# Three extra weight pairs that join a ring at the start of a stage: an encoder layer on Trainium2

## The chip, the core and the metric

The kernel runs on one core of one Trainium2 chip. The core has five engines that run at the same time, each with its own instructions in a fixed order: TensorE (PE, with its weight loads shown as PEld) multiplies matrices, VectorE (DVE) and ScalarE (ACT) work elementwise, GpSimd (POOL) does little else here than start transfers, and SyncE (SP) starts most of the transfers from memory (HBM). The metric is the time of one execution in microseconds (us).

## The reference, cut to what matters

One layer on 256 rows of width 2048: a half-weighted SwiGLU FFN of inner width 5632, a mixer (a state-space group and an attention group), a second such FFN, and a last gated stage ("ple"). What the change touches is the second FFN and the last stage:

```python
x = x + 0.5 * swiglu(rms_norm(x, ffn2_norm[i]), ffn2_w_gate[i], ffn2_w_up[i], ffn2_w_down[i])

gate = jax.nn.sigmoid(rms_norm(x, ple_norm[i]) @ w_ple_gate[i])
e = (p[i] @ w_ple_proj[i]) * gate
x = x + rms_norm(e, ple_post_norm[i])

def swiglu(h, w_gate, w_up, w_down):
    return (jax.nn.silu(h @ w_gate) * (h @ w_up)) @ w_down
```

All of it is in float32. The result has 256 x 2048 values.

## The kernel before

**A product in three passes.** TensorE takes operands of a rounded type. Each float32 matrix is therefore split in two parts: `hi`, the value cast to that type by ACT (`split`, L182), and `lo`, the rest `src - hi` by DVE (L185). A product is then `hi*hi + lo*hi + hi*lo`, three matrix multiplications. The parts of a weight are a *weight pair*: `whi` and `wlo`, each 128 x 1024 numbers, that is two blocks of 128 x 512.

**How weights come in.** A weight block of 512 x 512 (1 MB) is loaded by SP into a tile called `raw` (L369, L585). The pool `wp` has 5 such tiles; late in the kernel two of them hold the rows of x, so that three are left for weights. A load has to wait until the tile's old content has been read for the last time, which is by the DVE instruction that makes the `lo` part of its second half. Each `raw` gives two weight pairs.

**The ring.** `weight_pair` gives out the tiles for a pair. Four pairs (`whi`, `wlo`) lie in `wp`. While the list `ring` holds a pool, three more pairs (`shi`, `slo`) lie in that pool, and the seven are given out in turn: `i % 7` of 1, 3 and 5 are the extra ones. A pair can be filled again when TensorE has read its old content. When the pool of a stage closes (`sums_phase`), `ring[0]` becomes None, and pairs come from the four of `wp` alone until a stage sets the ring again. Before the change that happened in `Seven.chunk`, at the first group of seven products of a stage.

**Columns and sevens.** Much of the FFN uses a scheme that saves one product in eight (`class Seven`): a 2 x 2 block product is made from seven products of sums of blocks (`chunk`). For it DVE also adds weight blocks (`add`, L578: `t1`, `t2`, `t4`), and one sum is made by POOL as an accumulating transfer (L671). In a chunk the seven products run in the order 1, 5, 6, 4, 2, 3, 7, each with six matrix multiplications of 512 columns and one weight pair. The rest of the block product is done plainly (`column`, through `gemm_half`, L386 and L379): there a weight pair serves twelve matrix multiplications.

**The last stage.** It begins with two columns (side 0, then side 1), each with one `raw` tile, so with four weight pairs, called c1 to c4 here (c1 and c2 from `raw_2780`, c3 and c4 from `raw_2788`). Then comes one chunk, whose weights are `raw_2802` and `raw_2803`; its pairs are called z1, z5, z6, z4, z2, z3, z7 after their products, and the next columns' first pair is n1. The chunk's left operand needs sums of the normalised rows, `whole` (L507) and `rows` (L524), and their parts `hhi` and `hlo`. The normalised rows themselves come from x by a DVE transpose into `mid` (L220), 16 small transfers by SP (L233, `h<-mid`), and a scaled split (L195 on ACT, L197 on DVE). ACT also squares x (L488) and scales a gain row `pg` (L114). The second FFN begins in the same way: two columns, then a chunk.

**What sets the order.** The Python order is not what each engine gets. A scheduling layer places the instructions of each engine in an order of its own, by when it expects operands and tiles to be there; what is marked with `pin` keeps its place. Tiles of a stage's pool lie where the tiles of the pools closed before lay, and each waits until those have been read.

Of the kernel before, what the change touches and what calls it, by code (L numbers as in the profile page):

```python
# [33 lines left out]
def layer_kernel(ctx: ExitStack, tc: tile.TileContext, a: dict, shapes: dict, out: bass.AP):  # L34
# [28 lines left out]
    def uid(s):  # L63
        count[0] += 1
        return f"{s}_{count[0]}"
# [7 lines left out]
    def phase(name):  # L73
        return tc.tile_pool(name=name, bufs=1, reuse_waits="tile")
# [10 lines left out]
    def halves(kind):  # L85

        return [
            actp.tile([P, 4, T], F32R, tag=kind + s, name=uid(kind + s), bufs={"n": 4, "h": 2}[kind])
            for s in ("hi", "lo")
        ]  # L90
# [17 lines left out]
    def put_off(steps, fn, *args):  # L108


        def g():
            for _ in range(steps):
                yield
            fn(*args)  # L114

        return start(g())

    def pin(ins):
        return tc.keep_in_program_order(ins)
# [59 lines left out]
    def split(hi, lo, src, scale=None, pinned=False):  # L179

        if scale is None:
            copy = nc.scalar.copy(hi, src)  # L182
            if pinned:
                pin(copy)
            rest = nc.vector.tensor_tensor(out=lo, in0=src, in1=hi.bitcast(F32), op=ALU.subtract)  # L185
            rests.append(rest.ins)
            copies.append(copy.ins)
            return copy.ins, rest.ins
        else:
            split_each(hi.unsqueeze(1), lo.unsqueeze(1), src.unsqueeze(1), [scale])  # L190
# [149 lines left out]
    ring = [None, 0]  # L340
# [10 lines left out]
    @contextmanager  # L351
    def sums_phase(name):
        with phase(name) as pool:
            yield pool
            ring[0] = None
# [147 lines left out]
    def whole_rows(pool, parts, pinned=False):  # L503

        hi, lo = parts
        u = pool.tile([P, 2, NB], F32, tag="sum", name=uid("whole"), bufs=2)
        added = nc.vector.tensor_tensor(  # L507
            out=u.rearrange("p j n -> p (j n)"), in0=hi.bitcast(F32).rearrange("p j t -> p (j t)"),
            in1=lo.bitcast(F32).rearrange("p j t -> p (j t)"), op=ALU.add,
        )  # L510
        if pinned:
            pin(added)
        return u.rearrange("p j n -> p (j n)").rearrange("p (j x b) -> p j x b", j=4, b=32)

    def sum_forms(pool, u, kind="n"):

        sums = pool.tile([P, 2, NB], F32, tag="sum", name=uid("rows"), bufs=2)
        s = sums.rearrange("p j n -> p (j n)").rearrange("p (z j x b) -> p z j x b", z=4, j=2, b=32)
        (a11, a21), (a12, a22) = ([u[:, k : k + 2, 4 * t : 4 * t + 4] for t in range(TT)] for k in (0, 2))
        for z, (x, y, op) in enumerate((  # L520
            (a21, a22, ALU.subtract), (s[:, 0], a11, ALU.subtract),
            (a11, a21, ALU.subtract), (a12, s[:, 1], ALU.add),
        )):
            nc.vector.tensor_tensor(out=s[:, z], in0=x, in1=y, op=op)  # L524
        both = halves(kind)
        split(*both, sums.rearrange("p j n -> p (j n)").rearrange("p (z t) -> p z t", z=4))
        return both
# [175 lines left out]
    def ffn(i, xn, nxt, bg=None):  # L703
# [5 lines left out]
        sevens = pools.enter_context(sums_phase(f"sums{i}"))  # L709
        hp = pools.enter_context(phase(f"h{i}"))  # L710
        side = ExitStack()
        prep = bg(side) if bg else None
        turns = sevens
        sums = []
        mids = {}

# [13 lines left out]
        for f in range(NF):  # L730
# [3 lines left out]
            if prep and f == early:  # L734
# [3 lines left out]
                turns = pools.enter_context(phase(f"turns{i}"))  # L738
# [900 lines left out]

    n1, nm, n2, npl = Normed("ffn1_norm", load_turned), Normed("mix_norm"), Normed("ffn2_norm", kinds="hhnn", late=0), Normed("ple_norm", late=0)  # L1640
    ffn(1, n1, nm, s5_prep)

    w_in = a["w_in"]
# [75 lines left out]
    mix.close()  # L1719

    ffn(2, n2, npl)


# [27 lines left out]
    def sigmoid(sg, t, ps):  # L1751
        return nc.scalar.activation(sg[:, t * NB : (t + 1) * NB], ps, AF.Sigmoid, scale=npl.rs(t))
# [31 lines left out]
        crossed(s)  # L1784

    with sums_phase("sums3") as sevens:
        forms = {1: sum_forms(sevens, whole_rows(sevens, npl(1)), "h")}
        s = Seven(npl, forms.get, ((wg, 0), (wg, NB)), sevens, sevens)
        s.column(0, (0,))
        s.column(1, (0,))  # L1790
        s.chunk(1, shared)
        put_off(0, opened, s)
        s.column(0, (2,))
        s.column(1, (2,))
        s.column(0, (3,), True)
        put_off(0, gated, s)
        s.column(1, (3,), True)
        nc.vector.tensor_tensor(out=g1, in0=s.banks[3.8], in1=g1, op=ALU.add)
        for t in range(TT):
            sigmoid(g1, t, h1[t])  # L1800
# [180 lines left out]
```

## Time and profile before

| what | value |
| --- | --- |
| time, median of 3 runs | 1809.0 us (1808.81 to 1809.14) |
| the profiled execution | 1810.11 us, its span 1808.3 us, granted clock 0.999 |
| busy: PE, PEld, DVE, ACT, POOL | 1801.0, 1492.8, 1614.2, 1081.4, 137.1 us |
| second FFN in the trace | PE from about 1021 to 1701 us |
| last stage in the trace | PE from 1701.19 us to the end |

A start in the trace's list of instructions is counted from the beginning of the span. Two matrix multiplications of one engine overlap in such a list (each is shown as 0.39 us long, while a new one starts about every 0.227 us), so a wait of TensorE is read from the distance between starts rather than from idle time.

### The profile page before, as it was taken

How to read it: one execution, taken by the hardware profiler on the slowest of the kernel's cores; microseconds unless marked ns; L12 is line 12 of the kernel's file. 1: busy time of each engine (PE TensorE's matmuls, PEld its weight loads, DVE VectorE, ACT ScalarE, POOL GpSimd, SP SyncE). 2: the span in 40 equal slices, each digit the busy share in tenths (PEclk: the TensorE clock that was granted, in tenths of full speed). 3: DMA queues.
4: the chain of work that ended last, by engine and by line, in shares of the span. 5: the costliest groups of instructions: out<-in, count | busy, mean ns of one | idle time of the engine just before them, and what ended most of it. 6: DMA issues, size and time to landing. Idle time of an engine off the chain costs nothing.

```text
span 1808.3 us, 24274 instructions
## 1 busy us (share of the span) xinstructions
PE 1801.0 (100%) x8892; PEld 1492.8 (83%) x8892; DVE 1614.2 (89%) x1894; ACT 1081.4 (60%) x1264; POOL 137.1 (8%) x196
## 2 busy tenths in 40 slices
PE   9999999999999999999999999999999999999998
PEld 8888888888888878888898888888888888888887
DVE  7998889999999898887867899999999999989875
ACT  7445456555666566456895566555565566666664
POOL 0020100000000001112121000000000000000000
PEclk9999999999999999999999999999999999999999
DMA  9689967787776667765646777776767787666663
GB/s 377 214 277 315 279 220 234 242 268 220 257 248 228 209 237 229 258 244 179 204 153 209 248 278 239 266 263 222 233 232 248 236 273 244 231 209 221 206 245 128
DMA packets 108662, 430.49 MB, mean 238 GB/s; under 512 B 24608, under 2 KB 48576, under 8 KB 66144
## 3 DMA queue, kind: packets, MB, share of 16 engines
q1 hardware_dynamic: 96096, 390.10, 60.9%
q0 software_dynamic: 12160, 38.55, 10.0%
q8 instruction: 69, 1.13, 0.2%
q14 instruction: 49, 0.40, 0.1%
q10 hardware_dynamic: 288, 0.31, 0.1%
HBM read 372.41 MB, written 10.88 MB: 212 GB/s over the span
## 4 chain that ended last, share of the span: by engine, by line
PE 90%; DVE 4%; DMA 2%; issue 1%; SPq 1%; ACT 1%; DVEq 0%; ACTq 0%; POOL 0%; POOLq 0%
PE acc L386 29%; PE acc L379 15%; PE aux L386 13%; PE aux L379 7%; PE acc L567 5%; PE acc L572 5%; PE acc L570 5%; PE aux L570 3%; PE aux L567 3%; PE aux L572 3%; DMA raw<-in_ffn_w_down 2%; DVE wlo L185 1%; SPq L233 1%; DVE slo L185 1%; DVE sum L578 1%
## 5 line engine op out<-in xcount | busy, mean ns | idle before, releaser
L185 DVE TENSOR_TENSOR wlo<-raw,whi 128x1024 fp32r<-128x1024 f32 x478 | 576.3, 1221 | 96.7 <-ACT whi L182 94.6
L182 ACT CAST whi<-raw 128x1024 fp32r<-128x1024 f32 x478 | 495.2, 1050 | 267.2 <-PE acc L386 139.8
L386 PE MATMUL acc<-whi,nhi 128*128 128x512 f32 x850 | 331.7, 392 | 0.0
L386 PE MATMUL acc<-whi,nlo 128*128 128x512 f32 x850 | 329.7, 389 | 0.0
L379 PE MATMUL acc<-wlo,nhi 128*128 128x512 f32 x850 | 240.5, 389 | 0.1
L185 DVE TENSOR_TENSOR slo<-raw,shi 128x1024 fp32r<-128x1024 f32 x186 | 226.2, 1216 | 8.7 <-ACT shi L182 7.2
L182 ACT CAST shi<-raw 128x1024 fp32r<-128x1024 f32 x186 | 195.1, 1049 | 42.1 <-DMA raw<-in_ffn_w_down 22.5
L182 ACT CAST whi<-sum 128x1024 fp32r<-128x1024 f32 x83 | 87.5, 1054 | 168.8 <-DVE sum L578 159.3
L386 PEld LDWEIGHTS acc<-whi,nhi 128*128 128x128 f32 x850 | 159.7, 188 | 33.7 <-ACT whi L182 0.2
L379 PEld LDWEIGHTS acc<-wlo,nhi 128*128 128x128 f32 x850 | 159.4, 188 | 33.7 <-DVE wlo L185 0.5
L386 PEld LDWEIGHTS acc<-whi,nlo 128*128 128x128 f32 x850 | 159.6, 188 | 32.4
L182 ACT CAST shi<-sum 128x1024 fp32r<-128x1024 f32 x61 | 64.3, 1054 | 105.5 <-DVE sum L578 104.8
L671 POOL DMA_DIRECT2D raw<-raw x47 | 41.4, 880 | 1034.8 <-DVE sum L578 827.9
L578 DVE TENSOR_TENSOR sum<-sum,raw 128x1024 f32<-128x1024 f32 x96 | 117.1, 1220 | 0.9
L185 DVE TENSOR_TENSOR wlo<-sum,whi 128x1024 fp32r<-128x1024 f32 x83 | 101.2, 1221 | 3.1 <-ACT whi L182 2.2
L386 PE MATMUL aux<-whi,nhi 128*128 128x512 f32 x244 | 95.0, 389 | 0.0
L386 PE MATMUL aux<-whi,nlo 128*128 128x512 f32 x244 | 94.9, 389 | 0.0
L185 DVE TENSOR_TENSOR slo<-sum,shi 128x1024 fp32r<-128x1024 f32 x61 | 74.5, 1221 | 0.7
L379 PE MATMUL aux<-wlo,nhi 128*128 128x512 f32 x244 | 75.1, 389 | 0.0
L578 DVE TENSOR_TENSOR sum<-raw,raw 128x1024 f32<-128x1024 f32 x48 | 58.5, 1219 | 5.3 <-DMA raw<-in_ffn_w_down 5.2
L567 PE MATMUL acc<-whi,hhi 128*128 128x512 f32 x154 | 60.2, 391 | 0.0
L570 PE MATMUL acc<-whi,hlo 128*128 128x512 f32 x154 | 59.9, 389 | 0.0
(427 smaller groups left out, 3539.7 us busy)
## 6 DMA issues: line engine op xcount, KB each, us to landing
raw<-in_ffn_w_down SPq DMA_DIRECT2D x88, 1024.0 KB, 4.9
raw<-in_ffn_w_gate SPq DMA_DIRECT2D x87, 1024.0 KB, 7.3
raw<-in_ffn_w_up SPq DMA_DIRECT2D x87, 1024.0 KB, 5.6
raw<-in_w_in SPq DMA_DIRECT2D x32, 1024.0 KB, 5.7
raw<-raw POOLq DMA_DIRECT2D x50, 512.0 KB, 5.7
raw<-in_w_out SPq DMA_DIRECT2D x16, 1024.0 KB, 4.9
raw<-in_w_ple_gate SPq DMA_DIRECT2D x16, 1024.0 KB, 5.3
hT<-mid SPq DMA_DIRECT2D x160, 64.0 KB, 4.7
```

The costliest lines, as they stand in the source:

```text
L182: copy = nc.scalar.copy(hi, src)
L185: rest = nc.vector.tensor_tensor(out=lo, in0=src, in1=hi.bitcast(F32), op=ALU.subtract)
L233: nc.sync.dma_start(out[32 * q : 32 * q + 32].rearrange("p (t i w) -> p t i w", t=TT, i=4)[:, :, i], mid[32 * i : 32 * i + 32, q].rearrang ...
L379: nc.tensor.matmul(ps[t], lhsT=lh, rhs=lo[:, j, cols], start=False, stop=stop and j == 1, skip_group_check=joined,)
L386: nc.tensor.matmul(ps[t], lhsT=(ahi, alo)[i][:, 2 * h + j, t * P : (t + 1) * P], rhs=hi[:, j, cols], start=start and j == 0 and i == 0, st ...
L567: nc.tensor.matmul(ps, lhsT=lh[j], rhs=hi[:, j], start=begin and j == 0, stop=False, skip_group_check=joined)
L570: nc.tensor.matmul(ps, lhsT=ll[j], rhs=hi[:, j], start=False, stop=False, skip_group_check=joined)
L572: nc.tensor.matmul(ps, lhsT=lh[j], rhs=lo[:, j], start=False, stop=z in final and j == 1, skip_group_check=joined)
L578: nc.vector.tensor_tensor(out=t, in0=x, in1=y, op=ALU.add)
L671: nc.gpsimd.dma_start(b12, b22, accum_op=ALU.add)
```

## The change

Two places now set the ring: `ffn`, when it is the second FFN (`bg` is None), and the last stage, when its pool opens. `Seven.chunk` keeps its own line, which then finds the ring set.

```diff
@@ def ffn(i, xn, nxt, bg=None):
         side = ExitStack()
         prep = bg(side) if bg else None
         turns = sevens
+        if not bg:
+            ring[:] = [turns, 0]
         sums = []
         mids = {}
...
     with sums_phase("sums3") as sevens:
+        ring[:] = [sevens, 0]
         forms = {1: sum_forms(sevens, whole_rows(sevens, npl(1)), "h")}
         s = Seven(npl, forms.get, ((wg, 0), (wg, NB)), sevens, sevens)
         s.column(0, (0,))
```

No operation is added or taken away. In the second FFN the first four pairs now use tiles 0 to 3 of the ring of seven, and all later pairs of this stage are shifted by four places in it. In the last stage c2 and c4 move to extra tiles (`whi_2783` becomes `shi_2783`, `whi_2791` becomes `shi_2791`), z1 to a tile of `wp` that is not used by c1 to c4, and so on around the ring. TensorE's order stays the same row by row but for the tiles' names. DVE and ACT get another order in the second FFN and at the beginning of the last stage, and SP at the latter. Lines behind the edits move down by two or three: L1734 is L1736 after it, L1770 is L1772.

The first place is ACT at the beginning of the last stage. Before:

```order
L182 CAST whi_2781_14730<-raw_2780_14728 128x1024
L182 CAST hhi_2762_14652<-hT2_2084_11256 128x1024
L182 CAST whi_2783_14734<-raw_2780_14728 128x1024
L195 ACTIVATE nhi_2794_14794<-h_2747_14557,gains_90 128x256 x4
L182 CAST whi_2789_14773<-raw_2788_14771 128x1024
L182 CAST hhi_2778_14724<-rows_2777_14719 128x1024
L182 CAST whi_2791_14777<-raw_2788_14771 128x1024
L488 ACTIVATE sq_2796_14804,sm_7_113<-x_2394_12823 128x512
L488 ACTIVATE sq_2797_14806,sm_8_114<-x_2395_12824 128x512
L114 ACTIVATE pg_2769_14707<-pg_2769_14707 128x2048
L182 CAST whi_2805_14840<-raw_2802_14833 128x1024
```

And with the change:

```order
L182 CAST whi_2781_14730<-raw_2780_14728 128x1024
L182 CAST whi_2789_14773<-raw_2788_14771 128x1024
L182 CAST hhi_2762_14652<-hT2_2084_11256 128x1024
L195 ACTIVATE nhi_2794_14794<-h_2747_14557,gains_90 128x256 x4
L182 CAST whi_2805_14840<-raw_2802_14833 128x1024
L182 CAST shi_2783_14734<-raw_2780_14728 128x1024
L182 CAST shi_2791_14777<-raw_2788_14771 128x1024
L488 ACTIVATE sq_2796_14804,sm_7_113<-x_2394_12823 128x512
L488 ACTIVATE sq_2797_14806,sm_8_114<-x_2395_12824 128x512
L114 ACTIVATE pg_2769_14707<-pg_2769_14707 128x2048
L182 CAST hhi_2778_14724<-rows_2777_14719 128x1024
```

The cast of c2 has moved from before the scaled split `nhi` to behind it, and behind the cast of z1 (`whi_2805`), which reads the block `raw_2802`; the cast of c3 has moved forward, and that of `hhi` back.

The second place is DVE at the same point. Before:

```order
L185 TENSOR_TENSOR wlo_2784_14735<-raw_2780_14728,whi_2783_14734 128x1024
L197 SCALAR_TENSOR_TENSOR nlo_2795_14795<-h_2747_14557,gains_90,nhi_2794_14794 128x256 x3
L507 TENSOR_TENSOR whole_2776_14717<-nhi_2653_14097,nlo_2654_14098 128x1024
L197 SCALAR_TENSOR_TENSOR nlo_2795_14795<-h_2747_14557,gains_90,nhi_2794_14794 128x256
L524 TENSOR_TENSOR rows_2777_14719<-whole_2776_14717 128x256 x2
L524 TENSOR_TENSOR rows_2777_14719<-rows_2777_14719,whole_2776_14717 128x256
L524 TENSOR_TENSOR rows_2777_14719<-whole_2776_14717,rows_2777_14719 128x256
L185 TENSOR_TENSOR wlo_2790_14774<-raw_2788_14771,whi_2789_14773 128x1024
L185 TENSOR_TENSOR hlo_2779_14725<-rows_2777_14719,hhi_2778_14724 128x1024
L837 SCALAR_TENSOR_TENSOR x_2394_12823<-aux_2599_13803,x_2394_12823 128x512
```

And with the change:

```order
L185 TENSOR_TENSOR wlo_2790_14774<-raw_2788_14771,whi_2789_14773 128x1024
L185 TENSOR_TENSOR hlo_2763_14653<-hT2_2084_11256,hhi_2762_14652 128x1024
L197 SCALAR_TENSOR_TENSOR nlo_2795_14795<-h_2747_14557,gains_90,nhi_2794_14794 128x256 x4
L185 TENSOR_TENSOR wlo_2806_14841<-raw_2802_14833,whi_2805_14840 128x1024
L507 TENSOR_TENSOR whole_2776_14717<-nhi_2653_14097,nlo_2654_14098 128x1024
L185 TENSOR_TENSOR slo_2784_14735<-raw_2780_14728,shi_2783_14734 128x1024
L524 TENSOR_TENSOR rows_2777_14719<-whole_2776_14717 128x256
L839 SCALAR_TENSOR_TENSOR x_2394_12823<-aux_2599_13803,x_2394_12823 128x512
L839 SCALAR_TENSOR_TENSOR x_2395_12824<-aux_2599_13803,x_2395_12824 128x512
L524 TENSOR_TENSOR rows_2777_14719<-rows_2777_14719,whole_2776_14717 128x256
```

The rest of z1 (`wlo_2806`) now stands first after the four `nlo`, then `whole`, then the rest of c2; all that DVE did there before is behind them. Behind the rows shown the order of the change goes on with two more `rows`, two transposes (L220), the rest of c4 and `hlo_2779`.

The third place is DVE in the chunk that follows. Before:

```order
L578 TENSOR_TENSOR sum_2804_14837<-raw_2802_14833,raw_2803_14835 128x1024
L205 TENSOR_SCALAR sm_2799_14811<-sm_2798_14808 128x2
L185 TENSOR_TENSOR wlo_2806_14841<-raw_2802_14833,whi_2805_14840 128x1024
L578 TENSOR_TENSOR sum_2811_14862<-sum_2804_14837,raw_2803_14835 128x1024
L208 RECIPROCAL sm_2800_14813<-sm_2800_14813 128x2
L185 TENSOR_TENSOR pT1_14706<-sq_2841_15037,pT0_14705 128x512
L210 TENSOR_TENSOR sm_2801_14816<-sm_2800_14813 128x2
L185 TENSOR_TENSOR slo_2809_14852<-sum_2804_14837,shi_2808_14851 128x1024
L211 TENSOR_TENSOR sm_2801_14816<-sm_2801_14816,sm_2799_14811 128x2
L185 TENSOR_TENSOR wlo_2813_14865<-sum_2811_14862,whi_2812_14864 128x1024
L212 TENSOR_SCALAR sm_2801_14816<-sm_2801_14816 128x2
L578 TENSOR_TENSOR sum_2815_14875<-sum_2811_14862,raw_2802_14833 128x1024
```

And with the change:

```order
L185 TENSOR_TENSOR hlo_2779_14725<-rows_2777_14719,hhi_2778_14724 128x1024
L578 TENSOR_TENSOR sum_2804_14837<-raw_2802_14833,raw_2803_14835 128x1024
L208 RECIPROCAL sm_2800_14813<-sm_2800_14813 128x2
L578 TENSOR_TENSOR sum_2811_14862<-sum_2804_14837,raw_2803_14835 128x1024
L210 TENSOR_TENSOR sm_2801_14816<-sm_2800_14813 128x2
L185 TENSOR_TENSOR slo_2809_14852<-sum_2804_14837,shi_2808_14851 128x1024
L211 TENSOR_TENSOR sm_2801_14816<-sm_2801_14816,sm_2799_14811 128x2
L185 TENSOR_TENSOR slo_2819_14892<-raw_2802_14833,shi_2818_14891 128x1024
L212 TENSOR_SCALAR sm_2801_14816<-sm_2801_14816 128x2
L185 TENSOR_TENSOR wlo_2813_14865<-sum_2811_14862,whi_2812_14864 128x1024
L213 TENSOR_TENSOR sm_2800_14813<-sm_2800_14813,sm_2801_14816 128x2
L578 TENSOR_TENSOR sum_2815_14875<-sum_2811_14862,raw_2802_14833 128x1024
```

Here `sum_2804` is t1, `sum_2811` t2 and `sum_2815` t4. Between t1 and t4 the rest of z1 and that of `pT` are gone, and the rest of z2 (`slo_2819`) has come in.

On SP the row of `pg` has moved between the loads of `raw_2802` and `raw_2803`. The load of `raw_2803` takes the tile of `raw_2780`, so that it waits for the rest of c2, which reads that block last, before the change and after it. Shortly before the last stage, DVE now makes the two transposes for `h_2747` one after the other, ahead of a rest of 128 x 1024 that stood between them.

## The prediction

> **What bounds the kernel now.** I read the page's busy times first, then windows of the second FFN, then TensorE's waits and its list of starts, and last the lists of the engines that it waits for. In the windows the columns are the stretch, the sum, and busy time (with instructions) of PE, PEld, DVE, ACT and POOL, then the clock, the DMA share and GB/s.
>
> ```profile
> PE 1801.0 (100%) x8892; PEld 1492.8 (83%) x8892; DVE 1614.2 (89%) x1894; ACT 1081.4 (60%) x1264; POOL 137.1 (8%) x196
> ...
> 1100.00:1200.00 100.00, 100.00 (x443) 82.81 (x442) 98.09 (x96) 58.38 (x61) 4.39 (x5) 1.00 0.71 230
> ...
> PE acc L567 <- ACT shi L182: 0.6, 1, 0.6
> ```
>
> TensorE is the bound. In the second FFN it starts 443 matrix multiplications in 100 us, one every 100/443 = 0.2257 us, at clock 1.00; twelve take 2.71 us and six 1.36 us. A hundred us without a stall is what a deeper ring could improve on, so only the few places where starts lie further apart can give time back. TensorE's own starts show them:
>
> ```profile
> 1036.77 0.39 PE L567 MATMUL acc<-whi,hhi 128*128 128x512 f32 x1
> 1037.13 0.72 PE L572 MATMUL acc<-slo,hhi 128*128 128x512 f32 x2
> 1037.70 0.40 PE L570 MATMUL acc<-whi,hlo 128*128 128x512 f32 x1
> ...
> 1701.19 0.39 PE L386 MATMUL acc<-whi,nhi 128*128 128x512 f32 x1
> ...
> 1703.91 0.39 PE L386 MATMUL acc<-whi,nhi 128*128 128x512 f32 x1
> ...
> 1715.70 0.61 PE L572 MATMUL aux<-wlo,hhi 128*128 128x512 f32 x2
> 1716.90 0.50 PE L567 MATMUL acc<-shi,nhi 128*128 128x512 f32 x1 [0.59 <-ACT shi L182]
> ...
> 1718.74 0.40 PE L567 MATMUL acc<-whi,nhi 128*128 128x512 f32 x1
> ...
> 1722.87 0.48 PE L386 MATMUL acc<-whi,nhi 128*128 128x512 f32 x1
> ...
> 1724.68 0.39 PE L386 MATMUL acc<-whi,nhi 128*128 128x512 f32 x1
> ```
>
> In the first chunk of the second FFN, 1036.77 to 1037.70 holds three start distances, 0.93 us instead of 0.68: a stall of 0.25, at a rest (`slo`) that DVE has just made. In the last stage the two multiplications at 1715.70 make z4 due at 1716.15; it starts at 1716.90, 0.75 late, and its six take 1716.90 to 1718.74 = 1.84 instead of 1.36, 0.48 more. n1 takes 1722.87 to 1724.68 = 1.81, 0.45 more. So the last stage's start stalls by 0.75 + 0.48 + 0.45 = 1.68 us, and with the FFN's 0.25 everything that the change could win after 1000 us is 1.9 us.
>
> **The second FFN.** Nothing is added; the tiles of the pairs shift by four places. The first chunk's pairs find their tiles earlier, so I take the 0.25 stall as gone. Behind it there is nothing to win, and a loss would need DVE to come late; it was 98% busy from 1100 to 1200 with TensorE still never waiting. I count 0, with bounds of -0.25 (the stall's own size) and +0.5 (twice it, for one new stall elsewhere). Sum for this edit: -0.2.
>
> **The last stage: what waits for what.** ACT now casts z1 before c2 and c4, and z1's cast reads the block `raw_2802`, which is still on its way. So c2 and c4 are queued on ACT behind a transfer, and on DVE the rest of z1, at the head of everything, waits for that cast. The rows that price this are SP's, then ACT's:
>
> ```profile
> 1683.94 11.43 SPq L233 DMA_DIRECT2D h<-mid  x16
> 1695.47 1.00 SPq L585 DMA_DIRECT2D raw<-in_w_ple_gate  x2
> 1696.57 0.38 SPq L1734 DMA_DIRECT2D pg<-in_ple_post_norm  x1
> ...
> DMA to landing us min/median/max: 4.8/5.3/7.1
> ```
>
> ```profile
> 1696.91 1.71 ACT L195 ACTIVATE nhi<-h,gains 128x256 fp32r<-128x256 f32 x4 [3.08 <-DMA h<-mid]
> ...
> 1701.82 1.05 ACT L182 CAST hhi<-rows 128x1024 fp32r<-128x1024 f32 x1 [2.27 <-DVE rows L524]
> ...
> 1704.77 0.63 ACT L488 ACTIVATE sq<-x 128x512 f32<-128x512 f32 x1 [0.94 <-DVE x L837]
> ...
> 1706.15 1.90 ACT L114 ACTIVATE pg<-pg 128x2048 f32<-128x2048 f32 x1
> 1707.96 1.03 ACT L182 CAST whi<-raw 128x1024 fp32r<-128x1024 f32 x1
> ```
>
> And DVE's of the same stretch:
>
> ```profile
> 1697.46 1.28 DVE L197 SCALAR_TENSOR_TENSOR nlo<-h,gains,nhi 128x256 fp32r<-128x256 f32 x3 [2.37 <-ACT nhi L195]
> 1698.66 1.22 DVE L507 TENSOR_TENSOR whole<-nhi,nlo 128x1024 f32<-128x1024 f32 x1
> 1699.79 0.48 DVE L197 SCALAR_TENSOR_TENSOR nlo<-h,gains,nhi 128x256 fp32r<-128x256 f32 x1
> 1700.19 0.75 DVE L524 TENSOR_TENSOR rows<-whole 128x256 f32<-128x256 f32 x2
> ...
> 1701.65 1.22 DVE L185 TENSOR_TENSOR wlo<-raw,whi 128x1024 fp32r<-128x1024 f32 x1
> 1702.91 1.23 DVE L185 TENSOR_TENSOR hlo<-rows,hhi 128x1024 fp32r<-128x1024 f32 x1
> 1704.05 1.28 DVE L837 SCALAR_TENSOR_TENSOR x<-aux,x 128x512 f32<-128x512 f32 x2
> 1705.25 1.29 DVE L220 STREAM_TRANSPOSE mid<-x 128x512 f32<-128x512 f32 x2
> 1706.47 1.18 DVE L185 TENSOR_TENSOR wlo<-raw,whi 128x1024 fp32r<-128x1024 f32 x1
> ...
> 1707.70 1.21 DVE L578 TENSOR_TENSOR sum<-raw,raw 128x1024 f32<-128x1024 f32 x1
> ...
> 1709.03 1.22 DVE L185 TENSOR_TENSOR wlo<-raw,whi 128x1024 fp32r<-128x1024 f32 x1
> 1710.17 1.22 DVE L578 TENSOR_TENSOR sum<-sum,raw 128x1024 f32<-128x1024 f32 x1
> ...
> 1711.38 0.67 DVE L185 TENSOR_TENSOR pT<-sq,pT 128x512 fp32r<-128x512 f32 x1
> ...
> 1714.55 1.22 DVE L578 TENSOR_TENSOR sum<-sum,raw 128x1024 f32<-128x1024 f32 x1
> ```
>
> Instructions of one engine overlap a little, so I price by start distances: a rest or sum of 128x1024 costs DVE 1710.17 - 1709.03 = 1.14, the four `rows` 1701.65 - 1700.19 = 1.46, two additions to x 1.20, two transposes 1.22, `pT` 0.58; on ACT the two squares 1.38, `pg` 1.81, a cast 0.95 (1.05 until it can be used).
>
> **Step 1, the landing.** The load went out at 1695.47, behind the sixteen transfers of `h<-mid`. These may start one rest (1.14) earlier, since both transposes now stand ahead of it. With the median of 5.3 the block lands between 1699.6 and 1700.8; I take 1700.3, near the row's own time, because ACT, which starts `nhi` on those transfers, was still to be seen waiting 3.08 us for them.
>
> **Step 2, c2.** ACT casts z1 until 1701.35, c2 until 1702.3, c4 until 1703.25. DVE, with its `nlo` done by about 1699.1 (four at 0.4 from 1697.46), stands idle for 2.2 us, and then makes the rest of z1 from 1701.4, `whole` from 1702.53, and the rest of c2 from 1703.66 to 1704.88. c2's first multiplication is due at 1703.91, so its cast is in time; its rest is due four multiplications later, at 1703.91 + 0.90 = 1704.82. That is level: 0 to 0.5 late, and I count 0, since later lateness swallows it.
>
> **Step 3, t1.** After the rest of c2 DVE has the four `rows` (1.46), the additions to x (1.20) and the transposes (1.22): 1704.8 + 3.88 = 1708.68, then the rest of c4 until 1709.8, in time for its 1709.35 + 0.90 = 1710.25. ACT's squares need the first addition, which ends at about 1705.85: squares until 1707.23, `pg` until 1709.04, `hhi` until 1710.1. Only then can `hlo` run, from 1710.15, and t1's sum from 1711.28; before, it started at 1707.70. The block `raw_2803`, which t1 also needs, is loaded only when the rest of c2 is made: 1704.9 + 5.3 = 1710.2, just inside.
>
> **Step 4, z4.** From t1's sum to t4's sum DVE took 1714.55 - 1707.70 = 6.85. The rest of z1 (1.14) and that of `pT` (0.58) are gone from between, the rest of z2 (1.14) has come in: 6.27, so t4's sum starts at 1711.28 + 6.27 = 1717.55. Before, z4 started 1716.90 - 1714.55 = 2.35 after that start (the sum and the cast, and what lies between them), so it now starts at 1719.90, 3.75 later than due. z5's and z6's rests come late on the way (z6's is due at 1715.70 and ready at about 1717.5), but that is inside the 3.75. I add the same 0.48 for its six multiplications. n1's stall goes: TensorE reaches it 2.5 us later, and its block is there.
>
> Last stage: 3.75 + 0.48 - 1.68 = +2.55. With the FFN's -0.2 the sum is +2.3 us: a span of 1810.6 and a profiled execution of 1812.4 from 1810.11. That execution lay 1.1 above the median, so the median goes from 1809.0 to 1811.3.
>
> The largest unknown is the landing, since z4 follows it one to one. At 4.8 with the whole 1.14 gained it is 1699.2, 1.1 earlier: +1.2. At the late end it is a rival below. The rest of c2 0.5 late, or n1's 0.45 not won, gives +2.8.
>
> DVE is idle in step 2 while `whole` and the first of the `rows` could run; both stand behind the waiting rest of z1. Could they go ahead of it, 1.2 + 0.37 would leave the chain and the sum would be +0.7. The Trainium skill (Perfetto Trace Analysis, § Tensor Engine Instruction) says that ACT and DVE are strict first in, first out. By that page nothing goes ahead and the sum stays as it is; no run here shows the contrary.
>
> **The rivals.** *The block lands late, and the kernel is clearly slower.* The longest of these landings took 7.1 us. Then z1's cast ends 1.8 later, at 1703.15, c2's at 1704.1 (later than its 1703.91), and the rest of c2 at 1706.7, which puts the load of `raw_2803` off too; with 5.3 it lands at 1712.0, before t1's 1713.1, and with 7.1 at 1713.8. z4 comes 1.8 to 2.5 later than in the forecast: 1813.1 to 1813.8. For it: the place is new, and nothing covers it once the landing passes 1701.8. Against it: the 16 loads' median is 5.3.
>
> *A deeper ring removes the stalls.* With tiles free earlier, DVE and ACT make the pairs ahead; all 1.68 + 0.25 go, and the time is 1807.1. For it: ACT is only 60% busy, and the last stage's z4 stalls in the middle of a ring that has just grown. Against it: that wait is for a cast whose sum came off DVE at 1714.55, and on DVE nothing waited for a free tile. The Trainium skill (Perfetto Trace Analysis, § Optimization Strategy) says that the same gap repeating on the engine that should be saturated can mean too little on-chip memory for the next tile. By that rule seven pairs would help; the trace does not show its condition, since no gap repeats in 1100 to 1200.
>
> *Nothing moves.* The scheduling layer has only swapped work that was early: if ACT's `hhi` comes no later than needed and z4 starts within 0.5 of 1716.90, the time is about 1809.0. Against it: the idle 2.2 us of DVE ahead of work that is on z4's path.
>
> **How the numbers follow.** Forecast 0.60, at 1809.8 to 1812.4; the late landing 0.19; the stalls removed 0.11; nothing moves 0.08; a loss in the second FFN beyond its bound 0.02. The predicted time is the forecast's, 1811.3. The range 1808.5 to 1813.9 leaves out the 0.11 below and some 0.06 above. About 0.2% (3.6 us) is what a measurement can tell from no change. Faster than 1805.4 would need twice the stalls there are: 0.01. Slower than 1812.6 holds the late landing, the last case and a little of the forecast's upper end: 0.22. The same: 0.77.
>
> **What would show it.** In the changed trace: z1's cast on ACT waiting for the landing, ending at about 1701.3; DVE idle about 2 us before the rest of z1; ACT's `hhi` behind `pg` at about 1709; t1's sum at about 1711.3; and the stalls at z5's and z6's rests and at z4 some 3.7 us together, with n1 unstalled. The second FFN should still show 443 in 100 us. The prediction is wrong if TensorE reaches z4 without a wait, if t1's sum starts before 1709, or if a new stall stands between 1036 and 1700.

## The result, and the profile after

With the change the kernel takes 1811.7 us (median of 19 runs, 1808.6 to 1814.9), and before it 1808.6 in runs on the same chip: a ratio of 1.0020, with a 95% interval of 1.0014 to 1.0027. The change makes the kernel 3.1 us slower, and its runs lie further apart.

The two profiled executions differ by less, 1810.2 against 1808.3 us of span, because they differ by chance ahead of the second FFN as well: at the end of the first FFN (650 to 680 us), where both kernels are the same, TensorE lost 1.65 us in the execution of before that the prediction used, and nothing there in that of the change. So the stages are compared by the distance that TensorE needs from one multiplication to the same one later. The second FFN takes 0.8 us more, the last stage up to n1 2.4 us more, and from n1 on nothing differs: +3.2 us, about the difference of the medians. There is one trace of the kernel before, so what a stage of it takes is read from a single execution.

TensorE with the change, its view of waits and then its list of starts:

```profile
PE acc L567 <- ACT whi L182: 1.8, 2, 1.6
...
PE aux L572 <- DVE wlo L185: 0.7, 1, 0.7
```

```profile
1667.93 0.50 PE L386 MATMUL acc<-whi,hlo 128*128 128x512 f32 x1 [0.20 <-DVE hlo L185]
...
1673.61 0.50 PE L386 MATMUL acc<-whi,hlo 128*128 128x512 f32 x1
...
1716.19 0.73 PE L572 MATMUL aux<-wlo,hhi 128*128 128x512 f32 x2 [0.73 <-DVE wlo L185]
1718.48 0.51 PE L567 MATMUL acc<-whi,nhi 128*128 128x512 f32 x1 [1.55 <-ACT whi L182]
...
1724.78 0.50 PE L386 MATMUL acc<-whi,nhi 128*128 128x512 f32 x1 [0.22 <-ACT whi L182]
```

TensorE now stalls at z6's rest (1716.19), at z4 (1718.48) and again at n1 (1724.78); the two rows near 1670 are new small stalls at the end of the second FFN. What z4 waits for is read on the other engines, ACT first, then DVE and SP:

```profile
1695.06 1.71 ACT L195 ACTIVATE nhi<-h,gains 128x256 fp32r<-128x256 f32 x4 [3.45 <-DMA h<-mid]
1699.03 1.05 ACT L182 CAST whi<-raw 128x1024 fp32r<-128x1024 f32 x1 [2.26 <-DMA raw<-in_w_ple_gate]
1699.98 2.00 ACT L182 CAST shi<-raw 128x1024 fp32r<-128x1024 f32 x2
...
1706.02 1.90 ACT L114 ACTIVATE pg<-pg 128x2048 f32<-128x2048 f32 x1
1707.82 1.04 ACT L182 CAST hhi<-rows 128x1024 fp32r<-128x1024 f32 x1
...
1717.38 1.04 ACT L182 CAST whi<-sum 128x1024 fp32r<-128x1024 f32 x1 [2.66 <-DVE sum L578]
```

```profile
1700.11 1.23 DVE L185 TENSOR_TENSOR wlo<-raw,whi 128x1024 fp32r<-128x1024 f32 x1 [2.82 <-ACT whi L182]
1701.25 1.22 DVE L507 TENSOR_TENSOR whole<-nhi,nlo 128x1024 f32<-128x1024 f32 x1
1702.38 1.22 DVE L185 TENSOR_TENSOR slo<-raw,shi 128x1024 fp32r<-128x1024 f32 x1
...
1708.90 1.23 DVE L185 TENSOR_TENSOR hlo<-rows,hhi 128x1024 fp32r<-128x1024 f32 x1
1710.04 1.22 DVE L578 TENSOR_TENSOR sum<-raw,raw 128x1024 f32<-128x1024 f32 x1
...
1716.12 1.22 DVE L578 TENSOR_TENSOR sum<-sum,raw 128x1024 f32<-128x1024 f32 x1
```

```profile
1693.63 0.52 SPq L585 DMA_DIRECT2D raw<-in_w_ple_gate  x1
...
1703.63 0.33 SPq L585 DMA_DIRECT2D raw<-in_w_ple_gate  x1
```

The chain of the prediction is there link by link: the load of z1's block goes out at 1693.63, ACT is idle 2.26 us for it, DVE is idle 2.82 us behind ACT, `hhi` comes behind `pg`, and t4's sum starts 6.08 us after t1's.

To compare executions, the starts of t1's sum, z4 and n1 are counted from the start of c1's first multiplication. "z1's cast" is negative where ACT casts z1 before TensorE reaches c1, and empty where the cast waits for no landing.

| kernel (trace) | z1's cast | t1's sum | z4 | n1 |
| --- | --- | --- | --- | --- |
| before | | 6.5 | 15.7 | 21.7 |
| the change | -1.70 | 9.31 | 17.74 | 24.05 |
| the change, second trace | -1.20 | 9.80 | 18.23 | 25.76 |
| z1's block loaded in halves | -3.02 | 8.31 | 16.74 | 23.77 |
| `hhi` ahead of `pg` | -2.87 | 7.84 | 14.96 | 21.75 |
| `hhi` ahead of `pg`, second trace | -2.19 | 8.51 | 15.22 | 21.72 |
| z1's cast behind c4's | | 7.08 | 14.96 | 20.45 |
| last stage's edit alone | | 7.08 | 14.96 | 20.40 |
| second FFN's edit alone | | 5.53 | 14.96 | 20.40 |
| second FFN's edit alone, second trace | | 6.10 | 14.96 | 21.53 |

Without a stall z4 starts at 14.96 and n1 at 20.40.

### The profile page after: what moved, and what is told of

Read it like the earlier page. It is cut to its first block, busy times and chain, and to the rows that moved or that the text cites. A ratio compares the mean times of both kernels' runs of the same rounds, so it can differ in the third digit from the quotient of the medians.

```text
span 1810.2 us, 24268 instructions
## 1 busy us (share of the span) xinstructions
PE 1801.0 (99%) x8892; PEld 1491.1 (82%) x8892; DVE 1613.7 (89%) x1894; ACT 1080.6 (60%) x1264; POOL 137.1 (8%) x196
## 4 chain that ended last, share of the span: by engine, by line
PE 93%; DMA 3%; DVE 2%; issue 1%; SPq 1%; ACT 0%; DVEq 0%; ACTq 0%
PE acc L386 29%; PE acc L379 14%; PE aux L386 14%; PE aux L379 7%; PE acc L572 5%; PE acc L567 5%; PE acc L570 5%; PE aux L567 3%; PE aux L572 3%; PE aux L570 3%; DMA raw<-in_w_ple_gate 1%; DVE wlo L185 1%; DMA raw<-raw 1%; DMA raw<-in_ffn_w_gate 1%; SPq L233 1%
## 5 line engine op out<-in xcount | busy, mean ns | idle before, releaser
L182 ACT CAST whi<-raw 128x1024 fp32r<-128x1024 f32 x473 | 489.5, 1049 | 265.1 <-PE acc L386 139.8
L185 DVE TENSOR_TENSOR slo<-raw,shi 128x1024 fp32r<-128x1024 f32 x191 | 232.3, 1216 | 10.8 <-ACT shi L182 10.4
L182 ACT CAST shi<-raw 128x1024 fp32r<-128x1024 f32 x191 | 200.2, 1049 | 47.8 <-DMA raw<-in_ffn_w_down 25.1
```

## The experiments

My theory was that of the prediction: with both edits ACT's cast of z1 stands ahead of those of c2 and c4, waits for a transfer, and all that DVE does for the chunk follows later. The rivals: each edit loses by itself; only `pg` ahead of `hhi` matters; or the difference is chance ahead of the second FFN.

### Each edit alone

The second FFN's edit alone is the change without this line:

```diff
     with sums_phase("sums3") as sevens:
-        ring[:] = [sevens, 0]
```

> Only the second FFN's edit; the last stage sets its ring at the chunk as before. Here ACT casts c2 before everything and z1 behind the two squares, so no cast of the last stage's first four pairs stands behind a transfer. Theory (the loss lies in z1's cast standing ahead of c2 and c4, behind the landing of its block): no loss of the 2.5 us, a time within 1.5 us of the kernel before, most likely 0.2 to 1.5 us faster, since t4's sum also comes two instructions earlier. Rival (the second FFN's edit loses by itself; the trace of the change shows 0.6 us of new stalls at 1667 and 1673): slower than before by 0.5 us or more, with new stalls between 1650 and 1700.

The last stage's edit alone is the change without these:

```diff
         turns = sevens
-        if not bg:
-            ring[:] = [turns, 0]
```

> Only the last stage's edit. As the prediction put it, this edit alone carries +2.5 us: 1811 if the before is 1808.6. But the order that comes out of it is another than with both edits: ACT casts c2 and c4 before z1. Theory (the place of z1's cast is the cause, not the deeper ring): within 1 us of the kernel before or up to 1.5 faster. Rival (the deeper ring at the beginning of the last stage loses by itself): +2 to +3 us as with both.

| kernel | median (range) us, runs | ratio to before, 95% interval |
| --- | --- | --- |
| second FFN's edit alone | 1809.7 (1807.1 to 1813.0), 11 | 1.0008, 0.9999 to 1.0017 |
| last stage's edit alone | 1807.1 (1806.5 to 1809.2), 11 | 0.9996, 0.9987 to 1.0005 |
| both (the change) | 1811.7 (1808.6 to 1814.9), 19 | 1.0020, 1.0014 to 1.0027 |

The last stage's edit alone loses nothing. The prediction had put +2.55 us on this edit; its rival here (+2 to +3) is out. Its list of ACT shows why:

```profile
1697.37 1.71 ACT L195 ACTIVATE nhi<-h,gains 128x256 fp32r<-128x256 f32 x4 [2.76 <-DMA h<-mid]
1698.99 1.99 ACT L182 CAST shi<-raw 128x1024 fp32r<-128x1024 f32 x2
1701.09 1.05 ACT L182 CAST whi<-raw 128x1024 fp32r<-128x1024 f32 x1
```

c2 and c4 (the two `shi`) are cast first, z1 behind them. TensorE has no stall at all from c1 to the end of n1's six multiplications, that is 1.7 us less than before in this stretch. So the deeper ring does help here, and the order that the scheduling layer makes of both edits together takes it back and more. That the edit alone is faster is not shown: its interval includes 1.

The second FFN's edit alone is +1.5 us in the median, just within what could be none; the gain of 0.2 to 1.5 us that I had thought most likely did not come. Its runs lie 5.9 us apart, where the 33 runs of the kernel before that were timed beside them lie 2.7 us apart. Its slowest execution was the one traced, and ahead of the second FFN, where the two kernels are the same, it took 3.6 us more than the trace of before; from there on it took 0.9 us less. A second trace of it stands below.

### hhi ahead of pg, and z1 behind c4

```diff
-        put_off(5, nc.scalar.activation, pg, pg, AF.Copy, 0.0, -0.5)
+        def scaled():
+            with tc.issue_after(marks[0]):
+                nc.scalar.activation(pg, pg, AF.Copy, 0.0, -0.5)
+
+        put_off(5, scaled)
```

`marks[0]` is the cast of `hhi`.

> Both edits; the scaling of pg may not start before ACT has cast hhi. ACT then casts hhi right behind the squares, and DVE has t4's sum three instructions behind t1's instead of five. z1's cast stays ahead of c2 and c4. In the trace of the change ACT's squares end at 1706.0 and the rows are ready at 1706.1, so hhi is cast until 1707.2, hlo follows the transposes at 1707.3, the rest of c4 until 1709.5, t1's sum starts at about 1709.7 (from 1710.0) and t4's sum 3.5 later, at 1713.2 (from 1716.1). Theory (z4 is late by t4's sum): z4's pair is ready at about 1715.5, when TensorE gets there, and the time is 2.0 to 2.8 us below the change, about that of the kernel before. Rival (the landing ahead of c2 is all that matters): no more than 0.5 us below the change.

```diff
-            self.product(1, whole(0, 0), b11, final)
+            if self.ahead:
+                with tc.issue_after(self.ahead[0]), tc.issue_after(self.ahead[1]):
+                    self.product(1, whole(0, 0), b11, final)
+            else:
+                self.product(1, whole(0, 0), b11, final)
```

`ahead` holds the cast and the rest of c4, for the last stage's chunk alone.

> Both edits; in the last stage z1's cast may not start before those of c2 and c4 and their rests. Nothing of the first four pairs then waits for the landing. pg stays ahead of hhi. Theory (the landing ahead of c2 and c4 costs what DVE idles, 2.8 us in the trace of the change, less what TensorE's own last product of the second FFN holds back): t1's sum 0.5 to 1.5 us earlier, and t4's sum one instruction (1.1 us) closer to it since the rest of z2 has moved behind it: 1.5 to 2.5 us below the change. It also takes the landing's own variation out, so its runs should lie closer together than those of the change (1808.6 to 1814.9). Rival (pg ahead of hhi is all that matters): within 0.5 us of the change, with the same spread.

With z1's cast behind c4's the kernel takes 1808.1 us (1807.1 to 1810.4, 11 runs), a ratio of 1.0002 with an interval of 0.9993 to 1.0011, which does not meet that of the change. The loss is gone with this one constraint (more than the 1.5 to 2.5 us expected), and the runs lie 3.4 us apart instead of 6.4 (11 and 19 runs). Its ACT, DVE and TensorE:

```profile
1696.25 1.98 ACT L182 CAST shi<-raw 128x1024 fp32r<-128x1024 f32 x2
1698.15 1.05 ACT L182 CAST whi<-raw 128x1024 fp32r<-128x1024 f32 x1
```

```profile
1697.90 1.22 DVE L507 TENSOR_TENSOR whole<-nhi,nlo 128x1024 f32<-128x1024 f32 x1 [1.04 <-PE aux L379]
1699.04 1.22 DVE L185 TENSOR_TENSOR slo<-raw,shi 128x1024 fp32r<-128x1024 f32 x1
...
1707.50 1.22 DVE L579 TENSOR_TENSOR sum<-raw,raw 128x1024 f32<-128x1024 f32 x1
```

```profile
1715.38 0.39 PE L568 MATMUL acc<-whi,nhi 128*128 128x512 f32 x1
```

DVE makes `whole` at 1697.90, 1.04 us idle before it instead of 2.82, t1's sum starts 2.2 us earlier against c1 (7.08 for 9.31), t4's sum stands one rest nearer to it, and z4 (1715.38) is met without a wait. So the constraint moves two things, DVE's idle time and the place of t4's sum, and the time does not tell them apart. In its one trace the kernel takes 1.4 us less than before from the second FFN on, which its median does not show.

With `hhi` ahead of `pg` the median is 1811.8 us (1809.0 to 1814.6; ratio 1.0023, 1.0014 to 1.0032): no gain, where 2.0 to 2.8 us below the change had been expected. By its time this kernel does what the rival said. Yet both of its traces, this one and a later one, show z4 at 15.0 and 15.2, and a stretch up to n1 that is as long as before's. Both traced executions (1809.0 and 1807.8) lie at or below the fastest of the eleven. In this kernel t4's sum stands 3.64 us behind t1's instead of 6.08, so t4's nearer place, with z1's cast still ahead, does not bring the time back. What the usual execution of this kernel loses is in no trace here and stays open; that its z1 still waits for a landing fits, but is not shown to be the reason.

### The kernel cut to its end

To leave out chance ahead of the second FFN, four kernels were cut: the first FFN and the mixer are gone, x comes from memory, and the out-projection runs on a stand-in.

> The kernel before without the first FFN and the mixer: x is read from memory, the eight blocks of the out-projection run on a stand-in, and then come the second FFN and the last stage with their order unchanged. It is the base for the other three: some 890 us (787 from the second FFN's begin, about 90 for the out-projection, the rest start), and its runs close together (within 2.7 us, as those of the whole kernel were).

> The change, cut in the same way (without the first FFN and the mixer). Theory (what the trace shows: +0.8 us in the second FFN and +2.4 us at the last stage's beginning): 2.0 to 3.5 us above the cut kernel before, and a wider spread. Rival (a good part of the difference of the medians lies ahead of the second FFN, where the traces differ by -1.7 to +2.7 us at the same instructions): within 1 us of the cut kernel before, with a like spread.

> The second FFN's edit alone, cut in the same way (without the first FFN and the mixer). Its whole kernel was 1.5 us above the kernel before in the median, while its trace shows -0.9 us from the second FFN on and +3.6 us ahead of it. Theory (ahead of the second FFN is chance): 0 to 1 us below the cut kernel before. Rival (the second FFN's other order loses by itself in most executions): 1 to 2 us above it.

> Both edits with hhi cast ahead of pg's scaling, cut in the same way (without the first FFN and the mixer). The whole kernel was 3.7 us above the kernel before in the median, while its trace, of its fastest execution, shows -0.2 us from the second FFN on. Theory (z1's cast stands behind a landing that differs from execution to execution, the trace had a short one, 5.05 us): 1.5 to 3.5 us above the cut kernel before, with a wide spread. Rival (t4's earlier sum makes up for it, and the rest is chance ahead of the second FFN): within 0.7 us of the cut kernel before.

| cut kernel | median (range) us, runs |
| --- | --- |
| before | 891.4 (890.5 to 892.0), 4 |
| the change | 899.2 (896.7 to 901.4), 4 |
| second FFN's edit alone | 895.3 (894.0 to 897.0), 4 |
| both, `hhi` ahead of `pg` | 896.7 (893.3 to 897.9), 5 |

The rival that all of it is chance ahead of the second FFN is out: without all of that, the change still loses, and its runs are spread over 4.7 us where the kernel before has 1.5. But the sizes, +7.8 and +3.9 us, and +5.3 with `hhi` first, are far more than expected, and not those of the whole kernel. The waits of the change, cut, show where:

```profile
PE acc L567 <- ACT whi L182: 3.0, 2, 1.5
PE aux L572 <- DVE wlo L185: 1.2, 2, 0.6
```

Each of these stands there twice: once at the last stage's z6 and z4, and once at the second FFN's first chunk, which came right behind a beginning that the cut kernel alone has. From the traces' starts, about 2.9 us of the difference arise at that first chunk, 1.1 us at the end of the second FFN and 3.4 us at the last stage. In the whole kernel no trace shows the first of these. Part of the sizes comes after the stalls: the granted clock is 0.50 from 118.7 to 122.1 us and from 804.8 to 808.2, right behind the two places. So the cut kernels say that a loss arises behind the out-projection, and in them the FFN's edit costs time too; they don't give the sizes of the whole kernel.

### The landing as a dose

```diff
-                nc.sync.dma_start(raw, quarter(w, kb, n0))
+                if self.other and not raws:
+                    for h in range(2):
+                        nc.sync.dma_start(raw[:, 2 * h : 2 * h + 2], quarter(w, kb, n0)[:, 2 * h : 2 * h + 2])
+                else:
+                    nc.sync.dma_start(raw, quarter(w, kb, n0))
```

The condition holds for the first block of the last stage's chunk alone.

> Both edits; the first gate block of the chunk is loaded in two halves, the half with z1's weights first. The order of ACT and DVE at the last stage's beginning stays as with the change, z1's cast stays ahead of c2's and waits for 512 KB instead of 1 MB. Theory (all behind z1's cast follows its block's landing one to one): the cast starts earlier than 5.4 us after the load's issue, by 0.5 to 1.5 us if the half lands sooner, and t1's sum, z4 and the time come earlier by as much: 0.5 to 1.5 us below the change. Rival (the landing is not what sets z4): the same time as the change, also when the half lands sooner.

It takes 1811.2 us (1809.5 to 1813.7, 11 runs; ratio 1.0016, 1.0007 to 1.0025). The change had 1.0020 (1.0014 to 1.0027), and the intervals don't tell the two apart. The trace tells more:

```profile
1692.09 1.00 SPq L588 DMA_DIRECT2D raw<-in_w_ple_gate  x2
```

```profile
1696.66 1.05 ACT L182 CAST whi<-raw 128x1024 fp32r<-128x1024 f32 x1 [1.42 <-DMA raw<-in_w_ple_gate]
```

```profile
1716.43 0.50 PE L568 MATMUL acc<-whi,nhi 128*128 128x512 f32 x1 [1.55 <-ACT whi L182]
...
1723.46 0.50 PE L386 MATMUL acc<-whi,nhi 128*128 128x512 f32 x1 [1.15 <-ACT whi L182]
```

z1's cast starts 1696.66 - 1692.09 = 4.57 us after the issue; with the change it was 5.40 and, in the second trace, 5.02. The load also went out 0.5 us earlier against c1 than in the first trace of the change. Across the table, z1's cast, t1's sum and z4 move together: from the change to its second trace by 0.50, 0.49 and 0.49; to the halved load by -1.32, -1.00 and -1.00; between the two traces with `hhi` first by 0.68 and 0.67 (cast and sum). That is, nearly one to one, what the theory says of t1 and z4. It does not reach the end in full: with the halved load z4 comes 1.0 us earlier, but n1 waits 1.15 us for its own block, and starts only 0.3 us earlier. By these traces the rival, that the landing doesn't set z4, is out; by the times alone it is not.

### Second traces

Three of the kernels once more.

> The change once more, for a second trace. In the cut kernel a stall of 1.9 us at z4 was followed by multiplications that start every 0.427 us instead of every 0.227, for up to 3.6 us; in the first trace of the change a stall of the same size was not. Theory (the late z4 also costs time afterwards, in some executions, and this is what spreads the runs from 1808.6 to 1814.9): a run above 1812.5 shows such a stretch after z4 or another stall from the second FFN on; one below 1811 shows none. Rival (the spread comes from ahead of the second FFN): the second FFN and the last stage differ by less than 0.7 us from the first trace, whatever the time.

> Both edits with hhi cast ahead of pg, once more, since its first trace was of its fastest execution (1809.0 of 1809.0 to 1814.6) and showed -0.2 us from the second FFN on against the kernel before. Theory (z1's cast waits for a landing that differs): a run near its median of 1811.8 shows the loss at the last stage's beginning, z1's cast starting later than 5.05 us after the load's issue, or a stretch at 0.427 us. Rival (chance ahead of the second FFN): the trace from the second FFN on is again within 0.5 us of the kernel before.

> The second FFN's edit alone, once more; its first trace was of its slowest execution and lost 3.6 us ahead of the second FFN. The cut kernel showed stalls of 0.4 to 0.6 us each at the end of the second FFN (four of them) and more at its first chunk. Theory (this edit loses in the second FFN in some executions, up to the 0.8 us that the change's trace shows there and more at the first chunk): new stalls at the first chunk (about 1036 us) or between 1650 and 1680. Rival (all of its +1.5 us is chance ahead of the second FFN): none of these.

The change's second trace is of an execution of 1812.5 us. Its windows (the stretch, its length, PE, PEld, DVE, ACT, POOL, then the granted clock, DMA share and GB/s) and its list of TensorE:

```profile
1716.00:1720.00 4.00, 2.38 (x8) 1.35 (x9) 2.89 (x3) 2.91 (x3) 0.00 (x0) 1.00 0.72 243
1720.00:1723.20 3.20, 3.20 (x9) 2.50 (x8) 1.66 (x2) 0.04 (x1) 0.00 (x0) 0.50 0.69 233
1723.20:1727.00 3.80, 3.80 (x18) 3.12 (x17) 2.70 (x4) 3.78 (x7) 0.00 (x0) 0.97 0.98 406
```

```profile
1718.18 0.50 PE L567 MATMUL acc<-whi,nhi 128*128 128x512 f32 x1 [1.55 <-ACT whi L182]
...
1720.03 0.63 PE L567 MATMUL acc<-shi,nhi 128*128 128x512 f32 x1
1720.45 0.63 PE L570 MATMUL acc<-shi,nlo 128*128 128x512 f32 x1
...
1723.02 0.58 PE L570 MATMUL aux<-whi,hlo 128*128 128x512 f32 x1
1723.43 0.39 PE L567 MATMUL aux<-whi,hhi 128*128 128x512 f32 x1
```

z4 waits as long as in the first trace. But from 1720.03 to 1723.43 the granted clock is 0.50, and eight multiplications start every 0.427 us instead of every 0.227: 8 x 0.20 = 1.6 us more. The last stage loses 3.6 us in this execution and 2.4 in the first; the second FFN loses nothing here (-0.1) and 0.8 us there. So the same stall costs more in some executions than in others, which is part of why the runs of the change are spread. It is not all: such a stretch takes 0.0009 off the mean granted clock of an execution, and 8 of the change's 19 runs, the two longest (1814.7 and 1814.9 us) among them, list a mean of 1.000, which leaves no room for one. What those two lost is in no trace. With `hhi` ahead of `pg` 9 of 11 runs list 1.000, again with the two longest among them, so its loss is not this one either.

The FFN's edit alone, second trace: 1809.1 us, no loss ahead of the second FFN, +0.2 us in it and -0.1 after it; n1 waits 1.0 us. Small new stalls at 1672 us are there, none at the first chunk. Over all traces of kernels with this edit the second FFN takes between 0.3 us less and 0.8 us more than before.

## Why the prediction held, and where it did not

The forecast was 1811.3 us and +2.3; the runs gave 1811.7 and +3.1 (1.0014 to 1.0027). The direction, the place and the chain up to z4 were right. That the sizes fit so well is in part luck. The base of 1809.0 was 0.4 us above the median of more runs, which hides half of what the difference is short by. And in the last stage, forecast +2.55 and measured +2.4 in the first trace, two errors cancel: z4 comes 1.0 us less late than forecast, and n1 loses 0.85 us that the forecast had let go. One of the three signs that the prediction had named for being wrong did appear, new stalls between 1036 and 1700 us. The other two did not: TensorE waits at z4, and t1's sum starts after 1709. Step by step:

**The landing.** Right as a cause: with z1's cast behind c4's the loss is gone, and in the traces z4 follows z1's cast. Counted from c1, the load went out 1.4 us earlier than in the trace of before (7.1 us ahead of c1 instead of 5.7) in the first trace of the change and 0.5 us earlier in the second, where I had taken 0.5. ACT started z1's cast 5.40 and 5.02 us after the issue, for the 5.3 assumed.

**c2.** Right: its rest was made at 1702.38 to 1703.6, in time, so no stall stands at the first two columns in any trace.

**t1's sum.** Forecast 10.1 us after c1's start, measured 9.31 and 9.80: `hhi` did come behind the squares and `pg`, and `hlo` behind `hhi`, and the block came 0.8 and 0.3 us earlier against c1 than I had assumed, which is the whole difference.

**z4.** From t1's to t4's sum 6.08 us for the forecast 6.27, and 2.36 from there to z4 for 2.35. z4 is late by 17.74 - 14.96 = 2.78 and 3.27 us, where I had 3.75: the term was 0.5 to 1.0 too large, by the landing (0.3 and 0.8) and by 0.2 between the two sums.

**n1.** Wrong. The prediction let the 0.45 us at n1 go, since TensorE comes later and "its block is there". With the change n1 still loses 0.38 us at its first multiplication (0.604 us to the start before it, for 0.227) and 0.47 in its six. In the second trace n1 has no stall, but there TensorE came 1.6 us later still, at half clock. SP and ACT of the kernel before:

```profile
1706.69 9.45 SPq L233 DMA_DIRECT2D h<-mid  x12
1716.24 0.53 SPq L369 DMA_DIRECT2D raw<-in_w_ple_gate  x1
```

```profile
1721.74 1.05 ACT L182 CAST whi<-raw 128x1024 fp32r<-128x1024 f32 x1 [3.00 <-DMA raw<-in_w_ple_gate]
```

And of the change:

```profile
1707.39 8.69 SPq L233 DMA_DIRECT2D h<-mid  x12
1716.17 0.90 SPq L369 DMA_DIRECT2D raw<-in_w_ple_gate  x1
```

```profile
1723.68 1.05 ACT L182 CAST whi<-raw 128x1024 fp32r<-128x1024 f32 x1 [3.36 <-DMA raw<-in_w_ple_gate]
```

In both kernels, n1's load stands behind twelve `h<-mid`, which come behind the two transposes, and with the change these come after the same late rest of c2. It went out 0.4 us later against c1 than before, and ACT could cast 7.5 us after the issue (1716.17 to 1723.68), where it took 5.5 us in the trace of before (1716.24 to 1721.74). Why the block took 2 us longer is not shown. The failed step is that I moved TensorE and left the next load, and its time to land, where they were.

**The second FFN.** Forecast -0.2 with bounds of -0.25 and +0.5. The stall of 0.25 us at 1037 us went down to about 0.15, and new stalls came at 1667 and 1673 us: +0.8 in the first trace, -0.1 in the second. The upper bound was too low, and the case beyond it had been given a chance of 0.02. The stall at 1667.93 waits for an `hlo` of DVE, and DVE is busy without a gap from 1643 us to that `hlo`; so it was late from further back, and what made it late is not shown.

**What was missed.** The half clock after the stall, 1.6 us in the execution where it was seen. And that neither edit alone shows the loss: the prediction priced the last stage's edit from an order that needs the other edit too. The orders quoted were those of both edits, so the forecast for the change stands, but the sentence that each edit has its own sum does not.

Of the rivals, the late landing (1813.1 to 1813.8 us) has the time of single runs, not of the median, and no trace shows it (z1's cast came 5.40 and 5.02 us after the issue, where the rival needs 7.1); the deeper ring that removes the stalls is what the last stage's edit does alone, as its trace shows, and not what both do; "nothing moves" is out.

## What to carry to other kernels

A deeper ring frees work to be placed earlier, and an in-order engine pays for it when what is placed earlier waits for a transfer: look at which instruction stands ahead of the urgent ones and what it waits for, not at how many tiles there are. Two edits that a scheduling layer sees together can give an order that neither gives alone, so each should be run alone. When a stall on the bound engine moves, follow the loads that its late neighbours release, since the next stall may be there.

## What the runs showed of the hardware

A stall of TensorE of under 2 us can cost more after it has ended. In the change's second trace, at z4, the start distance was 1.95 us (1.72 beyond the usual 0.227), with another 0.9 us lost just ahead of it at z6's rest; the granted clock then was 0.50 for 3.40 us, beginning 1.85 us after z4 had started. The change, cut, shows the same after the same stall, with starts up to 0.43 us apart until 808.25:

```profile
804.26 0.51 PE L567 MATMUL acc<-whi,nhi 128*128 128x512 f32 x1 [1.54 <-ACT whi L182]
...
805.31 0.63 PE L570 MATMUL acc<-whi,nlo 128*128 128x512 f32 x1
...
808.25 0.62 PE L572 MATMUL acc<-slo,nhi 128*128 128x512 f32 x2
```

In the first trace of the change the same two stalls were followed by no such stretch. At the first chunk of the cut kernels, a start distance of about 1.87 us stands in all three that have the FFN's edit; two of them have the clock at 0.50 for 3.4 us behind it, and the one with `hhi` first has 1.00. The Trainium skill (TensorE: Matmul & The Clock Gate, § What's actually happening) describes a gate that halves the clock after an idle window of about 3.4 us, in windows of that length which run on their own. The length of the stretch (3.40 us) agrees with it. So do the times at which the clock changes in the traces of this case: each lies a whole number of steps of 3.413 us behind the first change (in the second trace of the change at 6.50, 1719.99 and 1723.40 us, 502 and 503 steps). Windows that run on their own would explain why the same stalls trip it in some executions only, which no run here tests. The idle time does not agree: ahead of these stretches no start distance reached 2 us.

Short stalls also cost a little once more: the first two multiplications after a wait start 0.33 to 0.34 us apart instead of 0.227, in all the traces shown here.
